# MoBA and MLA mixers on Trainium2: the last head group's values computed per token tile, and paired score products kept together

## The chip, the core and the metric

The kernel runs on one NeuronCore of a Trainium2 chip. The metric is the device time of one execution in microseconds (us); lower is better. The median of three timed runs before the change is 1003.63 us (1003.06 to 1005.63).

The engines are called by the profile's short names: PE (TensorE, matrix products; PEld is its weight load), DVE (VectorE), ACT (ScalarE), POOL (GpSimd) and SP (SyncE, which issues the DMAs here).

## What is computed

A trunk of two layers over one sequence of 256 tokens, width 1024, all in f32. Each layer is half a SwiGLU feed-forward, a token mixer, and half a feed-forward; layer 0 mixes with MoBA attention, layer 1 with MLA attention. Every sub-layer norms its input and shifts, scales and gates it by vectors made from `c`.

```python
def reference(x, c, positions, ...):
    c_act = silu(c)
    for layer in range(2):
        sh1, sc1, g1, sh2, sc2, g2, sh3, sc3, g3 = split(c_act @ ada_w[layer] + ada_b[layer], 9)
        h = modulate(rms_norm(x, norm_g[layer, 0]), sh1, sc1)
        x = x + 0.5 * g1 * swiglu(h, w_gate, w_up, w_down)
        h = modulate(rms_norm(x, norm_g[layer, 1]), sh2, sc2)
        mix = moba_attention(h, ...) if layer == 0 else mla_attention(h, ..., shared_k, shared_v)
        x = x + g2 * mix
        h = modulate(rms_norm(x, norm_g[layer, 2]), sh3, sc3)
        x = x + 0.5 * g3 * swiglu(h, ...)
    return x
```

With 256 tokens and a MoBA block of 256 both mixers come to causal attention over 16 heads: scores of a query with the keys (MoBA adds a position bias), softmax, a weighted sum of the values (64 wide), and an output projection of 1024 by 1024. MoBA's queries and keys are 64 wide, MLA's 96.

## The kernel before

**Numbers and tiles.** The 256 tokens are two token tiles of 128, t0 and t1. Every f32 operand of a large product is held as two fp32r parts, `hi` (a rounded copy) and `lo` (the rest), and a product is three matmuls added up in PSUM: hi by hi (L758), hi by lo (L759) and lo by hi (L760), in `mm3`. Weights come by DMA from SP into `raw` tiles of 1 MB (three buffers, L735); ACT copies each half into `hi` (L628) and DVE subtracts to get `lo` (L629), in `split`. `hi` and `lo` have eight buffers each, so a new `hi` can be written when the matmuls of the one eight places before have read it. The vectors from `c` are made beside this from `adaw` tiles, on DVE (L639, L677).

PSUM's eight banks are four accumulators `mm`, three banks for transposes, scores and values (`tr` and `at`, one pool), and one (`ada`) that MoBA's scores use as a fourth.

**Attention.** `attention()` runs once for each of the four groups of four heads (NG = 4, GH = 4) of either mixer. `scores` multiplies queries and keys; in MoBA (the branch with a bias) the four heads' products go, by token tile and by even and odd head, into four banks (`sides`, L1024). An even head's queries use the first 64 rows of the array and an odd head's the other 64. DVE adds the bias and takes the extreme (L1039), ACT does the exponential (L1046), DVE divides by the sum (L1051, L1052). `transposes` turns the probabilities (L1061): one unit of four transposes for t0 and two units for t1, each into one bank that ACT copies out as `pT` (L1063). `av` multiplies with the values (L1081) into one bank for both token tiles, and `split_evac` takes that out as the `hi` (ACT, L773) and `lo` (DVE, L774) parts of `oT`, two of the eight row blocks (k) of the out projection's input.

**Out projection and what follows.** `out_proj` has four accumulators, one for each token tile and half of the columns. In MoBA `mm_657` and `mm_659` are the two halves of t0, `mm_658` and `mm_660` those of t1. The last two row blocks (k = 6, 7) of each need the last group's `oT`. When one is complete, `resid` multiplies it with the gate and adds it to x (DVE, L868 and L869), and `stat` adds up squares (ACT L787, DVE L790). When both halves of a tile are done POOL makes `rstd`, ACT scales x into `y` (L803), PE transposes y (L808), ACT modulates it (L826) and `split_evac` makes the `hi` and `lo` of `h` (L773, L774), the input of the next feed-forward, whose first matmul needs them.

**What sets the order.** The program is written in rough order with continuations (`later(S_WAIT, ...)`, `later(PT_WAIT, ...)`, `later(AV_WAIT, ...)`), and then `class Order` (L243) schedules it: it simulates all engines with a table of costs, places one instruction after the other on the engine that is free first, takes on PE the oldest one that has been ready for a while (`choose`), and pins the result. Each engine then runs its instructions in exactly that order, waiting where an input or a buffer isn't there. So a change in one place can move instructions on all engines.

Of the kernel before, what the change touches and what calls it, by code (L numbers as in the profile page):

```python
# [24 lines left out]
S = 256  # L25
NT = S // P
# [5 lines left out]
DH = 64  # L32
# [210 lines left out]
class Order:  # L243
# [1 line left out]

    def __init__(self, nc, tc, rank, held, late, anchor):
        self.tc, self.rank, self.held = tc, rank, held
        self.tiles = {t.name: t for t in tc.info.tiles}  # L250
        self.ins, self.pre, self.aps = [], [], []
        self.uses, self.opened = {}, {}
        closed, seen, masks = [], {}, {}
        for i in nc.cur_bb.bb.instructions:
            kind = type(i).__name__
            if kind == "BassTilePoolBoundary":
                if i.op == "release":
                    closed.append(i.bass_pool_name)
                else:
                    self.opened[i.bass_pool_name] = list(closed)  # L260
            elif kind != "InstRegisterMove":
                self.add(i, seen, masks)
        n = len(self.ins)
        self.eng = [i.engine.name for i in self.ins]
        self.dma = [type(i).__name__ == "InstDMACopy" for i in self.ins]
        self.cost = [duration(i, a) for i, a in zip(self.ins, self.aps)]
        self.table = [{"Silu": "s", "Sin": "s", "Exp": "e"}.get(str(getattr(i, "func", "")).rsplit(".", 1)[-1])
                      if e == "Activation" else None for i, e in zip(self.ins, self.eng)]
        self.succ, self.after = [[] for _ in range(n)], [[] for _ in range(n)]
        self.npre = [len(p) for p in self.pre]  # L270
        for j, p in enumerate(self.pre):
            for i in p:
                self.succ[i].append(j)
        index = {i.name: k for k, i in enumerate(self.ins)}
        for x in late:
            if x in index:
                self.after[index[anchor]].append(index[x])
                self.npre[index[x]] += 1

        self.ring, self.bufs, self.rings, self.next_tile = {}, {}, {}, {}  # L280
        self.tiles_of = [[] for _ in range(n)]
        pools = {p.name: p for p in tc.info.pools}
        for name, us in self.uses.items():
            t = self.tiles[name]
            if t.space == DRAM:
                continue
            tag = str(t.tag).rsplit("_", 1)[0]
            pool = max((p for p in pools if tag.endswith("_" + p)), key=len)
            r = self.ring[name] = pool, tag
            if r not in self.bufs:  # L290
                self.bufs[r] = pools[pool].tag_meta[tag[:-len(pool) - 1]].bufs
            l = self.rings.setdefault(r, [])
            if l and self.uses[l[-1]][0] != us[0]:
                self.after[self.uses[l[-1]][0]].append(us[0])
                self.npre[us[0]] += 1
            if len(l) >= self.bufs[r]:
                self.next_tile[l[-self.bufs[r]]] = name
            l.append(name)
            for u in us:
                self.tiles_of[u].append(name)  # L300
# [63 lines left out]
    def place(self, need):  # L364
# [29 lines left out]
        def consider(k):  # L394

            r = ready[k]
            for t in self.tiles_of[k]:
                if t not in granted:
                    waiting.setdefault(t, []).append(k)
                    if t not in asked:  # L400
                        asked[t] = True
                        grant(self.ring[t])
                    return
                r = max(r, granted[t] + (WAKE if granted[t] else 0.0))
            if self.ins[k].name in self.held:
                r = max(r, HELD)
            ready[k] = r
            heapq.heappush(known[self.eng[k]], (r, k))

        def choose(e, t):  # L410
            av = avail[e]
            if e == "PE":
                first = min(av)
                old = [x for x in av if x[2] <= t - (GATE_MARGIN if x[0] < 0 else MARGIN)]
                x = min(old) if old else min(av, key=lambda x: (x[0] < 0, x))
                if x is not first and first[2] <= t and order[e] and order[e][-1] in self.pre[first[1]]:
                    x = first
                return x
            x = min(av)
            for r, j in known[e]:  # L420
                if r < t + min(self.cost[x[1]][0], SOON) and need[j] < x[0] - 500.0:
                    fit = [y for y in av if t + self.cost[y[1]][0] <= r + 60.0]
                    if fit:
                        return min(fit)
                    if need[j] < t + 3000.0:
                        free[e] = r
                        return None
                    break
            return x
# [93 lines left out]
def trunk(ctx: ExitStack, tc: tile.TileContext, a: dict, out: bass.AP):  # L523
# [28 lines left out]
    def later(us, fn):  # L552
        uid[0] += 1
        bisect.insort(pend, (clock[0] + us, uid[0], fn))
# [24 lines left out]

    first_rank, held, late, last_ffn = {}, set(), set(), []

    @contextmanager
    def noted(names):
# [289 lines left out]
    def kslice(tile_, k):  # L875
        return tile_[:, k * P:(k + 1) * P]
# [124 lines left out]
    def attention(ap, g, qTs, kTs, vs, bias, oT, state, after_s=None):  # L1001
# [7 lines left out]
        def scores():  # L1009
            until(lambda: state.get("av", 0) >= g)  # L1010
            banks = []
            if bias is None:
                for t, es in us:
                    ps3 = at_tile().rearrange("p (e k) -> p e k", k=P * (t + 1))
                    for i, e in enumerate(es):
                        nc.tensor.matmul(ps3[:, i, :], qTs(e, t), kTs(e, P * (t + 1)), start=i == 0, stop=False)  # L1016
                    nc.tensor.matmul(ps3[:, :, t * P:], ident_b, mask[:, :len(es)], start=False, stop=True)
                    banks.append([ps3[:, i, :] for i in range(len(es))])
            else:
                sides = [at_tile() for _ in range(3)] + [ps_ada.tile([P, 512], F32, tag="ada", name=nm("at"))]  # L1020
                sides = [x.rearrange("p (e k) -> p e k", k=P * (i // 2 + 1)) for i, x in enumerate(sides)]
                for t in range(NT):
                    for e in range(GH):
                        nc.tensor.matmul(sides[2 * t + e % 2][:, e // 2, :], qTs(e, t), kTs(e, P * (t + 1)),  # L1024
                                         start=True, stop=True)
                banks = [[sides[2 * t + e % 2][:, e // 2, :] for e in es] for t, es in us]
            pe(3.0)
            mxs = []
# [27 lines left out]
        def transposes():  # L1056
            for u, (t, es) in enumerate(us):
                pt = at_tile()
                for i, e in enumerate(es):
                    for kb in range(t + 1):  # L1060
                        nc.tensor.transpose(kslice(pt, i * (t + 1) + kb), ss[u][:, i, kb * P:(kb + 1) * P], ident)  # L1061
                w = ap.tile([P, 512], F32, tag="w", name=nm("pT"), bufs=5)
                nc.scalar.activation(w, pt, AF.Copy)  # L1063
                for i, e in enumerate(es):
                    for kb in range(t + 1):
                        pT[t, e, kb] = kslice(w, i * (t + 1) + kb)
            pe(1.4)
            state["p"] = g + 1
            if after_s:
                after_s()  # L1070
            later(AV_WAIT, av)

        def av():
            until(lambda: state.get("v", 0) > g)
            po = at_tile().rearrange("p (r t q) -> p r t q", r=GH // 2, t=NT)
            for pr in range(GH // 2):
                for t in range(NT):
                    for i in range(2):
                        e = 2 * pr + i
                        for kb in range(t + 1):  # L1080
                            nc.tensor.matmul(po[i * DH:(i + 1) * DH, pr, t, :], vs(e, kb),  # L1081
                                             pT[t, e, kb], start=kb == 0, stop=kb == t)
            pe(2.4)
            kk = g * (GH // 2)
            pov = po.rearrange("p r t q -> p t r q")
            hi, lo = [oT[0][3][:, kk:kk + 2, i].rearrange("p r t q -> p t r q") for i in range(2)]
            split_evac(hi, lo, pov)
            for t in range(NT):
                oT[t][2].update((kk, kk + 1))
            state["av"] = g + 1  # L1090

        later(S_WAIT, scores)

# [538 lines left out]
    mla(dict(hnext), hkv, norm_to((1, 2)))  # L1632
    ffn(1, 1, dict(hnext), lambda t: None, 18)
    drain()
    Order(nc, tc, first_rank, held, late, last_ffn[0]).apply()


# [17 lines left out]
```

## Time and profile before

| | us |
|---|---|
| median of three timed runs | 1003.63 |
| lowest and highest of them | 1003.06, 1005.63 |
| the profiled execution, its own time | 1006.99 |
| span of that profile, first to last instruction | 1005.2 |

The profile is one execution, 3.36 us above the median of the timed runs; 1.8 us of its time lie outside the span. Its views are: the busy time of each engine; the waits of an engine, by what released it; the chain of waits, which follows what ended last backwards through time (each row: start, length, engine and line; a length there is the step from one instruction's start to the next, not its latency); the timeline of an engine, instruction by instruction, with the idle time before each in brackets; and windows, which give each engine's busy time and the clock that PE was granted in a stretch of time. Durations in the timeline overlap for matmuls, since they are pipelined: a 128x512 matmul is listed with 0.39 us but the next one starts 0.23 us later. An f32 product is run as two passes over its columns, so that 8 score products of a group are 16 entries in the profile.

### The profile page before, as it was taken

The page shows a single profiled execution, that of the slowest core. Times are in us where ns is not written, and L with a number is a line of the kernel's source. Part 1 is how long each engine was busy: PE and PEld are TensorE (multiplying, and loading weights), DVE is VectorE, ACT ScalarE, POOL GpSimd, SP SyncE. Part 2 cuts the span into 40 slices and gives each one's busy share as a digit, 9 for nine tenths or more (in the row PEclk, how much of TensorE's full clock was granted, in tenths as well). Part 3 has the DMA queues.
Part 4 walks back from the last instruction along what each step waited for, and adds up shares of the span by engine and source line. Part 5 has one row for each costly group of instructions (what it writes and reads, how often), then busy time and mean ns, then how long its engine had stood idle before and what let it go on. Part 6 is the DMA issues. An engine that isn't in the chain of part 4 may idle for free.

```text
span 1005.2 us, 15142 instructions
## 1 busy us (share of the span) xinstructions
PE 986.0 (98%) x5558; PEld 834.1 (83%) x5558; DVE 844.9 (84%) x1389; ACT 616.7 (61%) x1111; POOL 83.8 (8%) x120
## 2 busy tenths in 40 slices
PE   8999999999999999999999999999989999999998
PEld 6988788877777788888888888888878878888886
DVE  7999999799989899999889999744998789667642
ACT  5689565378666775555367555643879686556421
POOL 2012000022231000000000000000143110000000
PEclk9999999999999999999999999999999999999999
DMA  9979879798886789988988998552344467544630
GB/s 352 404 283 304 317 285 360 299 336 328 273 292 246 254 294 329 340 326 291 364 310 331 341 334 300 180 210 104 105 152 149 144 227 283 204 168 168 224 132 21
DMA packets 54235, 260.51 MB, mean 259 GB/s; under 512 B 6289, under 2 KB 6801, under 8 KB 35986
## 3 DMA queue, kind: packets, MB, share of 16 engines
q1 hardware_dynamic: 52850, 256.06, 70.3%
q0 software_dynamic: 1024, 3.17, 1.1%
q8 instruction: 43, 0.70, 0.3%
q10 hardware_dynamic: 288, 0.33, 0.1%
q14 instruction: 30, 0.25, 0.1%
HBM read 255.34 MB, written 4.19 MB: 258 GB/s over the span
## 4 chain that ended last, share of the span: by engine, by line
PE 76%; issue 11%; DMA 6%; DVE 5%; ACT 2%; POOL 1%; SPq 0%; POOLq 0%; ACTq 0%; DVEq 0%
PE mm L955 20%; PE mm L758 13%; PE mm L759 13%; PE mm L760 13%; PE mm L962 11%; DMA adaw<-in_ada_dram 2%; DMA bias_d<-bt 2%; DMA raw<-in_first_dram 1%; PE at L1081 1%; DVE lo L629 1%; PE at L1016 1%; PE at L1024 1%; PE tr L808 1%; DMA raw<-in_w_dram 1%; PE at L1061 1%
## 5 line engine op out<-in xcount | busy, mean ns | idle before, releaser
L629 DVE TENSOR_TENSOR lo<-raw,hi 128x1024 fp32r<-128x1024 f32 (+3 forms) x312 | 371.4, 1201 | 86.8 <-ACT hi L628 67.6
L628 ACT ACTIVATE hi<-raw 128x1024 fp32r<-128x1024 f32 (+3 forms) x312 | 316.4, 1039 | 153.9 <-PE mm L760 113.6
L955 PE MATMUL mm<-h,hi 128*128 128x512 f32 x1120 | 288.3, 394 | 2.5 <-DVE ry L967 1.8
L955 PEld LDWEIGHTS mm<-h,hi 128*128 128x128 f32 x1120 | 199.7, 189 | 37.8 <-DVE ry L967 2.1
L962 PEld LDWEIGHTS mm<-h,lo 128*128 128x128 f32 x1120 | 155.3, 190 | 11.9
L962 PE MATMUL mm<-h,lo 128*128 128x256 f32 x1120 | 162.0, 283 | 0.0
L639 DVE CUSTOM_DVE_ANT_0 adaw<-adaw,c_b,cols 128x1024 f32<-128x1024 f32 x112 | 141.6, 1279 | 1.6 <-DMA adaw<-in_ada_dram 1.6
L758 PE MATMUL mm<-hi,gh 128*128 128x512 f32 x352 | 137.3, 390 | 0.0
L760 PE MATMUL mm<-hi,gl 128*128 128x512 f32 x352 | 137.1, 389 | 0.0
L759 PE MATMUL mm<-lo,gh 128*128 128x512 f32 x352 | 137.0, 389 | 0.0
L966 ACT ACTIVATE both<-mm 128x256 f32<-128x256 f32 x108 | 40.6, 376 | 91.0 <-PE mm L962 90.6
L758 PE MATMUL mm<-hi,h 128*128 128x512 f32 (+1 forms) x240 | 94.9, 401 | 0.8 <-ACT h L773 0.8
L760 PE MATMUL mm<-hi,h 128*128 128x512 f32 (+1 forms) x240 | 93.5, 394 | 1.6 <-DVE h L774 1.6
L759 PE MATMUL mm<-lo,h 128*128 128x512 f32 (+1 forms) x240 | 94.9, 397 | 0.0
L760 PEld LDWEIGHTS mm<-hi,gl 128*128 128x128 f32 x352 | 66.1, 188 | 13.7
L759 PEld LDWEIGHTS mm<-lo,gh 128*128 128x128 f32 x352 | 66.1, 188 | 13.5
L758 PEld LDWEIGHTS mm<-hi,gh 128*128 128x128 f32 x352 | 66.1, 188 | 13.4
L677 DVE SCALAR_TENSOR_TENSOR acc<-adaw,cols,acc 128x1024 f32<-128x1024 f32 x48 | 61.5, 1280 | 0.1
L967 DVE TENSOR_TENSOR both<-both,mm 128x256 f32<-128x256 f32 x108 | 44.9, 416 | 14.4 <-ACT both L966 14.0
L760 PEld LDWEIGHTS mm<-hi,h 128*128 128x128 f32 x240 | 45.5, 190 | 10.4 <-DVE h L774 2.1
L758 PEld LDWEIGHTS mm<-hi,h 128*128 128x128 f32 x240 | 45.4, 189 | 9.7 <-ACT h L773 1.3
L759 PEld LDWEIGHTS mm<-lo,h 128*128 128x128 f32 x240 | 45.3, 189 | 9.0 <-issue 1.0
(234 smaller groups left out, 1182.7 us busy)
## 6 DMA issues: line engine op xcount, KB each, us to landing
raw<-in_w_dram SPq DMA_DIRECT2D x142, 1024.0 KB, 5.7
adaw<-in_ada_dram SPq DMA_DIRECT2D x160, 512.0 KB, 5.7
raw<-in_first_dram SPq DMA_DIRECT2D x24, 256.0 KB, 7.3
raw<-in_w_dram SPq DMA_DIRECT2D x12, 512.0 KB, 3.9
raw<-in_w_dram SPq DMA_DIRECT2D x6, 576.0 KB, 4.1
bias_d<-bt SPq DMA_DIRECT2D x12, 256.0 KB, 5.2
bg<-bias_d POOLq DMA_DIRECT2D x4, 768.0 KB, 7.6
raw<-in_w_dram SPq DMA_DIRECT2D x2, 768.0 KB, 4.1
```

Of the source, the lines that this page charges most:

```text
L628: nc.scalar.activation(hi, src, AF.Copy)
L629: nc.vector.tensor_tensor(lo, src, hi.bitcast(F32), op=ALU.subtract)
L639: nc.vector.tensor_tensor_reduce(wt, wt, c_b, 1.0, cols[:, i, c:c + 1], op0=ALU.mult, op1=ALU.add, accum_out=m_cols[:, i, c:c + 1])
L677: nc.vector.scalar_tensor_tensor(acc, ada_tile(j, k), cact[:, k:k + 1], acc, op0=ALU.mult, op1=ALU.add)
L758: nc.tensor.matmul(ps, lh, rh, start=start, stop=False)
L759: nc.tensor.matmul(ps, lh, rl, start=False, stop=False)
L760: nc.tensor.matmul(ps, ll, rh, start=False, stop=stop)
L808: nc.tensor.transpose(kslice(pt, j), kslice(y, j), ident)
L955: nc.tensor.matmul(ps, wh, hk_both(h, k).rearrange("p i t q -> p (i t q)"), start=k == 0, stop=False)
L962: nc.tensor.matmul(ps[:, S:], wl, hk_both(h, k)[:, 0].rearrange("p t q -> p (t q)"), start=False, stop=k == KD - 1)
L966: nc.scalar.activation(sums, ps[:, S:], AF.Copy)
L967: nc.vector.tensor_tensor(sums, sums, ps[:, :S], op=ALU.add)
```

## The change

It has two parts.

1. **Twins.** In MoBA's scores each odd head's product is tied to that of the even head before it. `Order` lets the even one wait for everything that the odd one needs, its PSUM tile too, and places the odd one right behind it on PE.
2. **The last group's values by token tile.** In the last group (g = NG - 1) of both mixers `av` is run twice: for t0 directly behind t0's transposes and its `pT` copy, and for t1 where `av` stood. Each has an `at` bank of its own and a `split_evac` of half the width, so that t0's row blocks 6 and 7 are marked as there before t1's transposes are written.

```diff
@@ Order.__init__
-    def __init__(self, nc, tc, rank, held, late, anchor):
+    def __init__(self, nc, tc, rank, held, late, anchor, twins):
...
         index = {i.name: k for k, i in enumerate(self.ins)}
+        self.twin = {index[a]: index[b] for a, b in twins}
+        for a, b in self.twin.items():
+            for i in self.pre[b] - self.pre[a] - {a}:
+                self.pre[a].add(i)
+                self.succ[i].append(a)
+                self.npre[a] += 1
@@ Order, consider(k)
-            for t in self.tiles_of[k]:
+            for t in self.tiles_of[k] + (self.tiles_of[self.twin[k]] if k in self.twin else []):
@@ Order, choose(e, t)
                 first = min(av)
+                if order[e] and order[e][-1] in self.twin:
+                    b = self.twin[order[e][-1]]
+                    for x in av:
+                        if x[1] == b:
+                            return x
+                    for r, j in known[e]:
+                        if j == b:
+                            free[e] = r
+                            return None
@@ attention(), scores()
                         nc.tensor.matmul(sides[2 * t + e % 2][:, e // 2, :], qTs(e, t), kTs(e, P * (t + 1)),
                                          start=True, stop=True)
+                        if e % 2:
+                            twins.append([i.name for i in nc.cur_bb.bb.instructions[-2:]])
@@ attention(), transposes()
                     for kb in range(t + 1):
                         pT[t, e, kb] = kslice(w, i * (t + 1) + kb)
+                if g == NG - 1 and u == 0:
+                    av([0])
             pe(1.4)
             state["p"] = g + 1
             if after_s:
                 after_s()
-            later(AV_WAIT, av)
+            later(AV_WAIT, lambda: av([1] if g == NG - 1 else [0, 1]))
 
-        def av():
+        def av(ts):
             until(lambda: state.get("v", 0) > g)
-            po = at_tile().rearrange("p (r t q) -> p r t q", r=GH // 2, t=NT)
+            n = len(ts)
+            po = at_tile()[:, :n * S].rearrange("p (r t q) -> p r t q", r=GH // 2, t=n)
             for pr in range(GH // 2):
-                for t in range(NT):
+                for j, t in enumerate(ts):
                     for i in range(2):
                         e = 2 * pr + i
                         for kb in range(t + 1):
-                            nc.tensor.matmul(po[i * DH:(i + 1) * DH, pr, t, :], vs(e, kb),
+                            nc.tensor.matmul(po[i * DH:(i + 1) * DH, pr, j, :], vs(e, kb),
                                              pT[t, e, kb], start=kb == 0, stop=kb == t)
-            pe(2.4)
+            pe(1.2 * n)
             kk = g * (GH // 2)
-            pov = po.rearrange("p r t q -> p t r q")
-            hi, lo = [oT[0][3][:, kk:kk + 2, i].rearrange("p r t q -> p t r q") for i in range(2)]
-            split_evac(hi, lo, pov)
-            for t in range(NT):
+            hi, lo = [oT[0][3][:, kk:kk + 2, i, ts[0]:ts[-1] + 1].rearrange("p r t q -> p t r q") for i in range(2)]
+            split_evac(hi, lo, po.rearrange("p r t q -> p t r q"))
+            for t in ts:
                 oT[t][2].update((kk, kk + 1))
-            state["av"] = g + 1
+            if ts[-1]:
+                state["av"] = g + 1
```

`twins` is passed through to `Order(nc, tc, first_rank, held, late, last_ffn[0], twins)`. The lines move by up to 20: the score product of L1024 becomes L1039, L1061 becomes L1078, L1081 becomes L1101, `mm3` L773 to L775, the `hi` split L643, `split_evac` L788 and L789, `y` L818.

How the order changes is shown at three places. The first is PE at the scores of MoBA's last group (tiles `at_685` and `at_686` are t0's even and odd heads, `at_687` and `at_688` t1's). Before:

```order
L1024 MATMUL at_685_3697<-kT_680_3666,qT_2786 128x128
L1024 MATMUL at_688_3700<-kT_680_3666,qT_2786 128x256
L1024 MATMUL at_686_3698<-kT_680_3666,qT_2786 128x128
L758 MATMUL mm_658_3596<-hi_621_3472,oT_2787 128x512
L1024 MATMUL at_685_3697<-kT_680_3666,qT_2786 128x128
L1024 MATMUL at_686_3698<-kT_680_3666,qT_2786 128x128
L1024 MATMUL at_687_3699<-kT_680_3666,qT_2786 128x256 x2
L1024 MATMUL at_688_3700<-kT_680_3666,qT_2786 128x256
```

and after the change:

```order
L1039 MATMUL at_685_3697<-kT_680_3666,qT_2786 128x128
L1039 MATMUL at_686_3698<-kT_680_3666,qT_2786 128x128
L1039 MATMUL at_685_3697<-kT_680_3666,qT_2786 128x128
L1039 MATMUL at_686_3698<-kT_680_3666,qT_2786 128x128
L1039 MATMUL at_688_3700<-kT_680_3666,qT_2786 128x256
L1039 MATMUL at_687_3699<-kT_680_3666,qT_2786 128x256 x2
L1039 MATMUL at_688_3700<-kT_680_3666,qT_2786 128x256
```

In the first list an even product of t0 is followed by an odd one of t1, an odd one of t0 and a large matmul; in the second the even and odd head of one tile stand side by side in all four pairs, and the large matmul has left. The other three groups of MoBA have the same two patterns.

The second place is PE between the transposes and the values of the same group, where `pT_709` belongs to t0 and `at_715` holds the values of both tiles. Before, from the last transposes on:

```order
L1061 MATMUL at_712_3789<-ident_90,s_693_3719 128x128 x4
L760 MATMUL mm_660_3598<-hi_662_3601,oT_2787 128x512
L1081 MATMUL at_715_3796<-pT_709_3780,v_559_3235 64x128 x2
L1081 MATMUL at_715_3796<-pT_711_3787,v_559_3235 64x128 x2
L758 MATMUL mm_660_3598<-hi_664_3605,oT_2787 128x512
L758 MATMUL mm_658_3596<-hi_667_3623,oT_2787 128x512
L1081 MATMUL at_715_3796<-pT_713_3794,v_559_3235 64x128 x2
L1081 MATMUL at_715_3796<-pT_709_3780,v_559_3235 64x128 x2
L1081 MATMUL at_715_3796<-pT_711_3787,v_559_3235 64x128 x2
L1081 MATMUL at_715_3796<-pT_713_3794,v_559_3235 64x128 x2
L759 MATMUL mm_660_3598<-lo_665_3606,oT_2787 128x512
```

and after, from the values of t0 (`at_710`) to those of t1 (`at_723`), the first five rows:

```order
L1101 MATMUL at_710_3782<-pT_709_3780,v_559_3235 64x128 x4
L1078 MATMUL at_711_3789<-ident_90,s_691_3715 128x128 x4
L1078 MATMUL at_713_3796<-ident_90,s_693_3719 128x128 x4
L775 MATMUL mm_660_3598<-hi_664_3605,oT_2787 128x512
L773 MATMUL mm_660_3598<-hi_664_3605,oT_2787 128x512
```

and, nine matmuls on, the values of t1 with what ends t0's second half:

```order
L775 MATMUL mm_659_3597<-hi_705_3761,oT_2787 128x512
L1101 MATMUL at_723_3834<-pT_712_3794,v_559_3235 64x128 x2
L1101 MATMUL at_723_3834<-pT_714_3801,v_559_3235 64x128 x2
L1101 MATMUL at_723_3834<-pT_712_3794,v_559_3235 64x128 x2
L1101 MATMUL at_723_3834<-pT_714_3801,v_559_3235 64x128 x2
L773 MATMUL mm_659_3597<-hi_705_3761,oT_2787 128x512
L774 MATMUL mm_659_3597<-lo_706_3762,oT_2787 128x512
L775 MATMUL mm_659_3597<-hi_705_3761,oT_2787 128x512
L774 MATMUL mm_660_3598<-lo_665_3606,oT_2787 128x512
```

The values of t0 have moved ahead of t1's transposes, and t0's k = 6, 7 matmuls (`mm_657` and `mm_659` with weights `hi_669` and `hi_705`) stand ahead of and around the values of t1. From the last `mm_659` matmul to the first y transpose there were 17 matmuls before, and there are 22 now.

The third place is ACT where the out projection ends (`hi_...` from `raw_...` are weight splits for the next feed-forward, `y_727` and `y_728` the first scaled x of t0). Before:

```order
L773 ACTIVATE oT_2787<-at_715_3796 128x2x2x128
L628 ACTIVATE hi_760_3968<-raw_757_3962 128x1024
L628 ACTIVATE hi_763_3986<-raw_762_3984 128x1024
L787 ACTIVATE ry_716_3817,ssq0_717_3820<-x0_101 128x512
L628 ACTIVATE hi_765_3990<-raw_762_3984 128x1024
L628 ACTIVATE hi_771_4021<-raw_770_4019 128x1024
L628 ACTIVATE hi_773_4025<-raw_770_4019 128x1024
L803 ACTIVATE y_727_3853<-x0_101,rstd_726_3851 128x256
L803 ACTIVATE y_729_3855<-x0_101,rstd_726_3851 128x256
L826 ACTIVATE y_727_3853<-tr_737_3888,m_cols_104 128x128
L773 ACTIVATE h_725_3850<-y_727_3853 128x128
```

and after:

```order
L802 ACTIVATE ry_716_3809,ssq0_717_3812<-x0_101 128x512
L788 ACTIVATE oT_2787<-at_723_3834 128x2x128
L643 ACTIVATE hi_761_3971<-raw_758_3965 128x1024
L643 ACTIVATE hi_764_3989<-raw_763_3987 128x1024
L643 ACTIVATE hi_766_3993<-raw_763_3987 128x1024
L818 ACTIVATE y_728_3856<-x0_101,rstd_727_3854 128x256
L818 ACTIVATE y_730_3858<-x0_101,rstd_727_3854 128x256
L818 ACTIVATE y_732_3860<-x0_101,rstd_727_3854 128x256
L841 ACTIVATE y_728_3856<-tr_738_3891,m_cols_104 128x128
L788 ACTIVATE h_726_3853<-y_728_3856 128x128
L841 ACTIVATE y_728_3856<-tr_738_3891,m_cols_104 128x128
L841 ACTIVATE y_730_3858<-tr_741_3912,m_cols_104 128x128
```

The first two y's stood behind the splits of `raw_770` and now stand ahead of those of the same tile (`raw_771` in the second list), which have moved behind the h's of t0; a third y stands ahead of the first modulation.

More of the change, by code (lines that the diff above doesn't have):

```diff
@@ L578, in drain @@
             run_next()
-    first_rank, held, late, last_ffn = {}, set(), set(), []
+    first_rank, held, late, last_ffn, twins = {}, set(), set(), [], []
     @contextmanager
@@ L1634, in trunk @@
     drain()
-    Order(nc, tc, first_rank, held, late, last_ffn[0]).apply()
+    Order(nc, tc, first_rank, held, late, last_ffn[0], twins).apply()
 def kernel(**inputs):
```

## The prediction

> **What bounds the kernel now.** I read the page first, then PE's waits, then windows over the stages that the change touches.
>
> ```profile
> PE 986.0 (98%) x5558; PEld 834.1 (83%) x5558; DVE 844.9 (84%) x1389; ACT 616.7 (61%) x1111; POOL 83.8 (8%) x120
> ```
>
> PE is busy for 98% of the span. A part of the change pays only if it takes time off PE itself, or off one of PE's few waits. Its waits, by line and releaser (us in total, how many, the longest):
>
> ```profile
> PE tr L808 <- ACT y L803: 1.8, 2, 1.5
> PE tr L1453 <- DVE kn L1488: 0.8, 2, 0.6
> PE mm L758 <- ACT h L773: 0.8, 2, 0.6
> ```
>
> The first and the third have their longest occurrence behind MoBA's out projection. The second lies in MLA between its groups. MoBA's attention itself is full:
>
> ```profile
> 244.00:260.00 16.00, 16.00 (x99) 12.55 (x98) 14.06 (x36) 13.38 (x29) 4.83 (x3) 1.00 0.82 288
> 260.00:290.00 30.00, 30.00 (x165) 24.04 (x164) 27.62 (x54) 17.26 (x34) 5.92 (x4) 1.00 0.85 297
> 290.00:312.00 22.00, 22.00 (x134) 17.49 (x132) 19.99 (x40) 14.40 (x31) 6.26 (x3) 1.00 0.77 263
> 312.00:332.50 20.50, 20.48 (x115) 15.76 (x113) 18.43 (x39) 13.07 (x29) 0.00 (x0) 1.00 0.66 236
> ```
>
> The columns are the window's length, then the busy time of PE, PEld, DVE, ACT and POOL, the granted clock, and the DMA share. In 88.5 us PE is busy for all but 0.02, and DVE for 14.06 + 27.62 + 19.99 + 18.43 = 80.1, which is 91%. So here PE's own work is the bound, with DVE close behind it.
>
> **Part 1, the score pairs.** The chain of waits has MoBA's first group, and later its last:
>
> ```profile
> 245.04 0.85 PE at L1024 x5
> 245.90 0.43 PE mm L758
> 246.33 1.28 PE at L1024 x10
> ...
> 312.25 0.85 PE at L1024 x5
> 313.10 0.43 PE mm L758
> 313.54 1.28 PE at L1024 x10
> 314.82 0.43 PE mm L759
> 315.25 0.24 PE mm L760
> ```
>
> All four groups read so. Three products take 0.85, a large matmul caught between them 0.43 where its likes take 0.23 or 0.24, and five products 1.28: 2.56 us, of which 0.23 is the matmul's own work. In the new order the eight stand in four pairs, and the matmul stands elsewhere. The ten passes of the x10 row show the price of pairs. They hold one pair of t0 and three products of t1, two of an even head and one of an odd. The even half of the array streams 2 x 128 + 4 x 256 = 1280 columns in 1.28 us, 1.0 ns a column with its start, and the odd half has room beside it. The three products that join are t1's second odd one, which fits into that room, and a second pair of t0, two passes of 128 columns: 0.26 us. So 1.28 + 0.26 + 0.23 = 1.77 replaces 2.56. That is **-0.79 us a group, -3.2 us in four**. If the added pair costs nothing it is 4 x 1.05 = -4.2; if the odd product finds room for half of its 2 x 256 columns only, another 0.26 a group is lost and it is -2.1. I take -3.2, because in the x10 row an odd product already runs in that room.
>
> PE's work in this stage covers the softmax chain. What has to be late for PE to wait? The last group's products ended at 314.82 and its first transposes came at 318.49, with 15 large matmuls between. Now there are 16, so the chain behind the products has 0.23 us more, and t0's bank is complete earlier inside the run. That cover doesn't shrink. What does shrink is the time for DVE's other work (splits, `adaw` columns), for which there is a rival below.
>
> **Part 2 in MoBA: transposes and values.**
>
> ```profile
> 307.77 1.51 PE at L1081 x24
> ...
> 318.49 0.44 PE at L1061 x4
> ...
> 321.19 0.80 PE at L1081 x8
> 321.99 0.66 PE mm L758 x2
> 322.65 1.24 PE at L1081 x16
> 323.89 0.43 PE mm L759
> ```
>
> The third group does its 24 value passes in 1.51. The last group took 0.80 + 1.24 = 2.04 in two pieces, because a transposed tile was late, and its x8 piece mixed t0 with one head of t1. Each piece is followed by a matmul of 0.43, 0.20 above 0.23. Now the pieces are t0 (8 passes) and t1 (16), each whole pairs, so I take 1.51 plus 0.1 for a second start. The t0 piece is followed by transposes, which keep their 0.44 for four, so one of the two breaks goes too. Sum: 2.04 - 1.61 = 0.43 and something of the 0.20. **I take -0.5**, between -0.2 (the pieces cost what they did, one break goes) and -0.75. The second `split_evac` adds an ACT and a DVE instruction of half width. On ACT it stands behind `pT_709` and two weight splits (1.06 each, by a row below), so its `hi` comes some 3.2 us after t0's transposes. PE has six matmuls (1.4), the values (0.5), eight transposes (0.9) and three matmuls (0.7) until it reads that `oT`: 3.5 us. It just fits, and I take nothing; a split that comes late uses the cover up, and then PE waits for as long as it is late.
>
> **Part 2 in MoBA: the wait behind the out projection.**
>
> ```profile
> 332.25 0.24 PE mm L760
> 332.51 1.06 ACT hi L628
> 333.57 0.41 ACT y L803
> 334.02 0.45 PE tr L808 x2
> 334.56 0.47 ACT y L826
> 335.05 0.32 ACT h L773
> 335.41 0.55 PE mm L758
> ...
> 332.51 1.06 ACT L628 ACTIVATE hi<-raw 128x1024 fp32r<-128x1024 f32 x1 [0.30 <-PE mm L760]
> ...
> 329.09 1.22 DVE L629 TENSOR_TENSOR lo<-raw,hi 128x1024 fp32r<-128x1024 f32 x1
> 330.23 0.68 DVE L868 TENSOR_TENSOR ry<-mm,gate 128x512 f32<-128x512 f32 x1
> ...
> 332.35 0.08 DVE L790 DVE_READ_ACCUMULATOR2_ANT ssq<- 128x1 f32 x1
> ...
> 332.52 0.55 POOL L795 TENSOR_TENSOR rstd<-ssq,mhalf 128x1 f32<-128x1 f32 x1 [25.11 <-DVE ssq L790]
> ```
>
> PE stops when its last out-projection matmul is done (332.5) and waits 1.5 for `y`, then 0.6 for `h` (the longest of the two rows of waits above): 2.1 us. Two things are late at once. `rstd` is there only at 333.07, and ACT is in a weight split that waited for the buffer freed by the very last matmul. The new order cuts both. The t0 accumulator is complete 22 matmuls ahead of the transposes instead of 17. DVE started on that accumulator at 330.23, behind a split of 1.22, and its squares ended at 332.4, after which POOL's 0.55 gives `rstd`; in the new order that split stands behind the squares. And ACT's last split ahead of `y` (`hi_766`) now waits for the matmul that has four others behind it (0.9 us). So y is ready 1.06 + 0.41 + 0.05 = 1.5 after that matmul, and PE idles 1.5 - 0.9 = 0.6. Behind it the third pair of transposes and a matmul fill most of the second wait; about 0.3 stays. **From 2.1 to 0.9: -1.2 us.** Ends: -2.1 (no wait left), and 0 (something else is late by as much).
>
> **Part 2 in MLA.** There the values stood together, and PE waited on nothing near them:
>
> ```profile
> 798.36 1.31 PE at L1061 x12
> ...
> 800.59 1.51 PE at L1081 x24
> ```
>
> The split only adds: a second start (0.1) and a second break (0.20) at the values, and a break (0.1) as the transposes part into 4 and 8. By the order, 20 large matmuls lie between t0's accumulator and the first y transpose instead of 23; at 0.23 they are 4.6 us, above the 332.4 + 0.55 + 0.41 - 330.23 = 3.1 that MoBA's chain from residual to y takes by the rows above, so nothing new waits there. **+0.4 us**, between +0.2 (one break) and +0.7 (0.80 + 1.24 as in MoBA instead of 1.51, and one break).
>
> **What the scheduler moves besides.** In MLA between the groups the `kn` transposes now come in one run, and two DVE splits stand behind `kn` that stood ahead of it, while one score unit comes seven matmuls later. The waits there are 0.8 us in all. They may go (-0.8), or a wait of seven matmuls (1.6) may come. **I take -0.3**, nearer to the row of 0.8. The feed-forwards are reordered in places, but in the same full PE.
>
> **Sum:** -3.2 - 0.5 - 1.2 + 0.4 - 0.3 = **-4.8 us**. On the profiled execution, 1006.99 (span 1005.2), that is 1002.2. The median of the timed runs stands 3.36 lower, so 1003.63 - 4.8 = **998.8 us**.
>
> **The clock.** The profiled execution has something that the timed ones need not have:
>
> ```profile
> 328.90:332.31 3.41, 3.41 (x16) 1.00 0.79 244
> 332.31:335.72 3.41, 1.31 (x6) 1.00 0.25 106
> 335.72:339.13 3.41, 3.41 (x11) 0.50 0.91 298
> 752.14:755.56 3.42, 1.97 (x14) 1.00 0.00 0
> ```
>
> The wait behind MoBA's out projection left PE busy for 1.31 of 3.41 us, and the granted clock was halved for the next 3.41: 1.7 us lost. A stretch with 1.97 busy was not followed by it. With 0.9 idle, 2.5 of 3.41 stay busy and the halving should go. The stretches' ends needn't fall alike in each execution, so I leave these 1.7 us out of the median's sum; with them the profiled execution would come to 1000.5. [...]
>
> **Rivals.**
>
> 1. *Only the pairs pay.* The wait for `y` stays 2.1, because another split or the later DVE order holds it, and MLA's moved score unit costs 0.6: -3.2 - 0.5 + 0.4 + 0.6 = -2.7, so 1000.9. For it: DVE has an `adaw` column newly between t0's two residuals, on a tile as large as that of the 1.22 row. Against it: PE still works at `mm_659` then. Chance 0.18.
> 2. *The pairs don't overlap*, as a semaphore comes between their halves: -1.6 is left, 1002.0. For it: four banks must all be free at once. Against: the pair in the x10 row runs so. Chance 0.06.
> 3. *DVE becomes the bound of MoBA's attention: slower.* Its 80.1 us have to fit into what was 88.5 and becomes about 84.8. If it can keep busy only as in the first window, 14.06 of 16.00 or 0.88, the stage takes 80.1 / 0.88 = 91.0, which is +2.5 instead of -3.7; with -1.2 and +0.1 for the rest that gives 1005.0. The point from which the kernel is slower is 80.1 / 89.6 = 0.89. Against it: PE waited for DVE nowhere here, and DVE reached 0.92 in the second window (27.62 of 30.00), which would still leave 87.0 and a gain of 2.6. Chance 0.08.
> 4. *More*: the median had a halved clock too, or the first two terms lie at their far ends: 994 to 996.6. Chance 0.11.
>
> **The numbers.** The forecast, 996.6 to 1000.5 about 998.8, has the 0.57 left. A range of 996.0 to 1002.2 leaves out most of rival 3, half of 4 and a little of 2: about 0.16. A measurement of this kernel can't tell less than 0.3%, 3.0 us, from no change. Below 1000.6 lie the forecast, rival 4 and a few of 1: faster 0.70. Above 1006.6 lies a part of rival 3: slower 0.06. The same: 0.24.
>
> **What would show it.** Right: MoBA's sixteen score passes in a row of about 1.5 us in the chain, all four groups; value pieces near 0.5 and 1.1; PE's wait `tr L808 <- ACT y` under 1; no halved clock near 332. Wrong: new waits of PE for DVE between 240 and 330 (rival 3), score passes over 2 us (rival 2), a wait of 1.5 still there (rival 1).

## The result, and the profile after

| | us |
|---|---|
| median of five timed runs with the change | 995.87 (995.11 to 999.07) |
| median of five runs of the kernel before, beside them | 1005.26 (1003.06 to 1005.73) |
| ratio | 0.9916, 95% interval 0.9903 to 0.9929 |
| span of the profile with the change | 994.1 |

The change makes the kernel 0.84% faster, 8.4 us of 1005 (7.1 to 9.7). The forecast was 4.8 us, 998.8; the median lies just below the range's lower end of 996.0.

From the page of the changed kernel, busy time by engine:

```profile
PE 979.9 (99%) x5558; PEld 831.1 (84%) x5558; DVE 844.2 (85%) x1391; ACT 615.5 (62%) x1113; POOL 77.7 (8%) x120
```

And its waits of PE (us in total, how many, the longest):

```profile
PE tr L1473 <- ACT s L1063: 1.6, 2, 1.4
...
PE mm L773 <- ACT h L788: 0.5, 2, 0.3
PE tr L823 <- ACT y L818: 0.2, 1, 0.2
PE tr L1473 <- DVE kn L1508: 0.2, 1, 0.2
```

PE was busy for 986.0 before and is for 979.9 now. The wait of 1.5 for `y` is gone (the 0.2 left is at another place), the longest for `h` has halved, and the longer of the two waits for `kn` in MLA is gone. The wait of 1.8 for `ry` ahead of MoBA is gone too, though every engine's order is the same there; more of that below.

The chain of waits of the changed kernel, at MoBA's first group, at the transposes of its second, and in its last:

```profile
243.07 1.51 PE at L1039 x16
244.58 0.43 PE mm L773
...
269.21 0.87 PE at L1078 x8
...
307.96 1.51 PE at L1039 x16
309.47 0.43 PE mm L774
...
315.16 0.59 PE at L1101 x8
315.75 1.02 PE at L1078 x8
...
319.53 1.07 PE at L1101 x16
320.61 0.43 PE mm L773
```

All sixteen score passes stand in one run of 1.51. The values take 0.59 and 1.07. The 0.20 that the first break cost is gone at the matmul, but the eight transposes that follow the values take 1.02, where the eight of the second group take 0.87; so most of it comes back there.

The timeline of the changed kernel behind the out projection, ACT, POOL and PE:

```profile
324.50 1.06 ACT L643 ACTIVATE hi<-raw 128x1024 fp32r<-128x1024 f32 x1 [0.49 <-PE mm L775]
325.47 1.29 ACT L818 ACTIVATE y<-x,rstd 128x256 f32<-128x256 f32 x3
...
323.91 0.55 POOL L810 TENSOR_TENSOR rstd<-ssq,mhalf 128x1 f32<-128x1 f32 x1 [20.83 <-DVE ssq L805]
...
326.35 0.60 PE L823 MATMUL tr<-ident,y 128*128 128x128 f32 x4
327.02 0.38 PE L823 MATMUL tr<-ident,y 128*128 128x128 f32 x2
327.68 0.50 PE L773 MATMUL mm<-hi,h 128*128 128x512 f32 x1 [0.28 <-ACT h L788]
```

The y transposes have no idle time before them. `rstd` was there at 324.46, 1.9 us ahead of them, and the split in front of `y` began at 324.50, when a matmul was done that had nine others between it and the transposes.

DVE stayed clear of being the bound. This is the sum line of four windows over MoBA's attention (242 to 325 us) of the changed kernel:

```profile
sum 83.00, PE 83.00 PEld 66.50 DVE 78.01 ACT 56.06 POOL 16.47; mean PE 20.75 PEld 16.62 DVE 19.50 ACT 14.02 POOL 4.12
```

PE works in every microsecond, with DVE at 78.01 / 83.00 = 94%.

**Three stretches** make profiles comparable. They are cut at the start of MoBA's first score product (244.97 in the profile before), at the first y transpose behind MoBA's out projection (334.02), at the first y transpose ahead of MLA (706.85), and at the end of the span; what comes before the first cut is left out. In us, from the rows of each profile:

| kernel | MoBA | behind it, and two feed-forwards | MLA and the rest |
|---|---|---|---|
| before | 89.05 | 372.83 | 298.3 |
| before, a second profile | 89.04 | 372.68 | 298.3 |
| with the change | 83.35 | 370.95 | 296.8 |
| twins alone | 86.19 | 372.83 | 297.9 |
| twins, split in MoBA only | 83.35 | 371.07 | 298.5 |
| twins, split in MLA only | 86.17 | 372.92 | 296.2 |
| full change, twins of the same half | 87.12 | 371.82 | 296.5 |
| twins alone, matmuls in the wait | 86.16 | 371.78 | 297.9 |
| MoBA's split, MLA's scores 1.0 later | 83.35 | 371.05 | 297.1 |
| MoBA's split, MLA's values 1.0 later | 83.35 | 370.98 | 298.3 |
| full change, MLA's scores 1.0 later | 83.35 | 371.05 | 298.0 |
| MoBA's split, MLA's scores 2.0 later | 83.37 | 371.06 | 297.6 |

With the change the three are -5.7, -1.9 and -1.5 us: 9.1 in the profile, beside 8.4 in the timed runs.

### The profile page after: what moved, and what is told of

Its sections match the earlier page's. It is cut to its first block, busy times and chain, and to the rows that moved or that the text cites. A ratio compares the mean times of both kernels' runs of the same rounds, so it can differ in the third digit from the quotient of the medians.

```text
span 994.1 us, 15134 instructions
## 1 busy us (share of the span) xinstructions
PE 979.9 (99%) x5558; PEld 831.1 (84%) x5558; DVE 844.2 (85%) x1391; ACT 615.5 (62%) x1113; POOL 77.7 (8%) x120
## 4 chain that ended last, share of the span: by engine, by line
PE 73%; DVE 10%; issue 10%; DMA 4%; ACT 2%; POOL 1%; SPq 0%; DVEq 0%; ACTq 0%; POOLq 0%
PE mm L970 21%; PE mm L773 12%; PE mm L775 12%; PE mm L774 12%; PE mm L977 11%; DVE lo L644 3%; DMA raw<-in_w_dram 2%; PE at L1101 1%; PE at L1078 1%; DMA adaw<-in_ada_dram 1%; PE tr L823 1%; DVE oh L1221 1%; DMA raw<-in_first_dram 1%; ACT hi L643 1%; DVE acc L692 1%
## 5 line engine op out<-in xcount | busy, mean ns | idle before, releaser
L643 ACT ACTIVATE hi<-raw 128x1024 fp32r<-128x1024 f32 (+3 forms) x312 | 315.8, 1038 | 157.9 <-PE mm L775 115.8
L773 PE MATMUL mm<-hi,gh 128*128 128x512 f32 x352 | 137.3, 390 | 0.0
L775 PE MATMUL mm<-hi,gl 128*128 128x512 f32 x352 | 137.1, 389 | 0.0
L773 PE MATMUL mm<-hi,h 128*128 128x512 f32 (+1 forms) x240 | 94.5, 400 | 0.5 <-ACT h L788 0.5
L775 PE MATMUL mm<-hi,h 128*128 128x512 f32 (+1 forms) x240 | 92.4, 391 | 1.4 <-DVE h L789 1.4
L775 PEld LDWEIGHTS mm<-hi,gl 128*128 128x128 f32 x352 | 66.1, 188 | 13.7
L773 PEld LDWEIGHTS mm<-hi,gh 128*128 128x128 f32 x352 | 66.1, 188 | 13.4
L775 PEld LDWEIGHTS mm<-hi,h 128*128 128x128 f32 x240 | 45.0, 188 | 10.3 <-DVE h L789 1.7
L773 PEld LDWEIGHTS mm<-hi,h 128*128 128x128 f32 x240 | 45.1, 188 | 10.1 <-issue 1.2
```

What stands on the lines that cost most here:

```text
L643: nc.scalar.activation(hi, src, AF.Copy)
L773: nc.tensor.matmul(ps, lh, rh, start=start, stop=False)
L775: nc.tensor.matmul(ps, ll, rh, start=False, stop=stop)
```

## The experiments

The letters A to J are the theories and rivals that the expectations name.

### The parts one by one

The twins alone: `transposes` and `av` as before.

```diff
-                if g == NG - 1 and u == 0:
-                    av([0])
...
-            later(AV_WAIT, lambda: av([1] if g == NG - 1 else [0, 1]))
+            later(AV_WAIT, lambda: av([0, 1]))
```

> The twins alone; the values of the last group stay together in both mixers. Theory A, that the parts add up as the two traces read (pairs -3.3 us, values and the wait behind MoBA's out projection -2.2 and -1.7 of clock, MLA -1.5): 3.3 us faster than before, a wait of 1.5 for y still there, MLA unchanged. Rival B, that the pairs only take the place of waits that the split of the values makes possible to remove: under 1.5 us faster, with new waits of PE in MoBA.

Measured: 1001.72, ratio 0.9968 (0.9955 to 0.9980), so 3.2 us faster. MoBA's stretch is 2.86 shorter. The four runs of scores give 4 x 0.82 = 3.3 (2.56 before; 1.51 and 0.23 for the matmul that left), and 0.5 is lost again in the wait for `y`, which has become 2.0:

```profile
PE tr L823 <- ACT y L818: 2.3, 2, 2.0
```

The timeline of the same kernel, ACT and POOL at that place:

```profile
325.21 2.95 ACT L643 ACTIVATE hi<-raw 128x1024 fp32r<-128x1024 f32 x3
...
327.87 0.56 POOL L810 TENSOR_TENSOR rstd<-ssq,mhalf 128x1 f32<-128x1 f32 x1 [24.84 <-DVE ssq L805]
328.46 0.91 ACT L818 ACTIVATE y<-x,rstd 128x256 f32<-128x256 f32 x2 [0.30 <-POOL rstd L810]
```

ACT's last split ended at 328.16, and `rstd` was there at 328.43: it came last, by 0.27, where before the change the split came last, by 0.50 (333.57 and 333.07). So without the split of the values both things are late; by these rows, having the later one in time would alone bring no more than 0.3 here, and 0.5 before the change. Theory A stands but for the length of the wait, B falls.

The split in MoBA only, with the twins (`bias` is there in MoBA alone); the split in MLA only is the same edit with `bias is None`:

```diff
-                if g == NG - 1 and u == 0:
+                if bias is not None and g == NG - 1 and u == 0:
...
-            later(AV_WAIT, lambda: av([1] if g == NG - 1 else [0, 1]))
+            later(AV_WAIT, lambda: av([1] if bias is not None and g == NG - 1 else [0, 1]))
```

> Twins, and the values split by token tile in MoBA only; MLA's order is that of before. Theory A: 3.3 + 2.2 = 5.5 us faster than before, 7.2 where the halved clock behind the out projection fell on the run before; no wait for y; MLA takes as long as before from 741 us on. Rival C, that MLA's 1.5 us in the trace are a difference between two executions, as the 2.0 us ahead of MoBA must be (the order is the same there): as fast as the full change.

Measured: 998.7, ratio 0.9932 (0.9919 to 0.9946), 6.8 us faster, between A's 5.5 and 7.2. MoBA's stretch falls by another 2.84, of which 2.04 is the whole wait for `y`; the rest lies in smaller pieces at the last groups. The stretch behind falls by 1.8. MLA stays at 298.5, and its `kn` wait of 0.6 is there. So C falls: MLA's gain comes with the other half of the change.

> Twins, and the values split in MLA only; up to MLA this is the order of the twins alone, in MLA that of the full change. Theory A: 1.5 us faster than the twins alone, all of it between the first score products of MLA and the last values, with the kn wait of 0.6 gone. My own prediction of before, in which the split costs MLA 0.4 and the scheduler gives 0.3: the same as the twins alone. Rival C: no difference either, with the 1.5 us gone in this profile.

Measured: 1000.68, ratio 0.9952 (0.9939 to 0.9964), 1.0 us less than the twins alone by the medians; the intervals of the two ratios overlap. The profile is plainer: the first two stretches are those of the twins alone, and MLA's is 296.2 against 297.9. Theory A stands: MLA gains. My forecast of no gain there is wrong.

### What a pair is

The twins tie heads that use the same half of the array (the profile lists a score product as `64*128`):

```diff
-                        if e % 2:
-                            twins.append([i.name for i in nc.cur_bb.bb.instructions[-2:]])
+                        if e >= 2:
+                            last = nc.cur_bb.bb.instructions
+                            twins.append([last[-3].name, last[-1].name])
```

> The full change, but the twins tie heads 0 and 2 and heads 1 and 3, which use the same half of the array: the eight products of a group still stand in one run without a large matmul between them. Theory A, that the gain is the overlap of an even with an odd head: the run takes 2.3 to 2.5 us instead of 1.51 and some 3.2 to 3.8 us of the change's gain are lost. Rival D, that it is the uninterrupted run: 1.5 us for the sixteen passes, and the gain stays within 0.8 us.

Measured: 1001.18, ratio 0.9960 (0.9948 to 0.9973); 4.4 us of the change's 8.4 are lost, somewhat more than A's 3.2 to 3.8; MoBA's stretch is 3.8 longer than with the change, and the one behind it 0.9, though PE has no wait left there. The scheduler did not keep one run, contrary to what I expected; a large matmul stands in it. From the chain of waits of this kernel, first group:

```profile
244.03 1.52 PE at L1039 x10
245.54 0.43 PE mm L773
245.97 1.06 PE at L1039 x4
247.03 0.43 PE mm L774
```

The first row is six products (twelve passes, of which the chain follows ten), the second the two that are left. Six products without an interruption take 1.52, as long as eight in even and odd pairs. So it is the pairing that counts, and D falls. With 1.52 + 1.06 these are even slower than before the change (0.85 + 1.28). The same eight products take 1.51 with the halves in turn and 1.52 + 1.06 in this order.

### The clock behind the wait

Eight matmuls that nobody reads fill the wait of the twins-alone kernel, pinned right ahead of the first y transpose; nothing else in the order differs.

```diff
+                if half and t == 0 and gate_key == (0, 1):
+                    pf = ps_ada.tile([P, 512], F32, tag="ada", name="fill").rearrange("p (c q) -> p c q", q=P)
+                    for i in range(8):
+                        nc.tensor.matmul(pf, ones_r, ones_r[:, None, :].to_broadcast([P, 4, P]), start=i == 0, stop=i == 7)
```

> The twins alone, with eight large matmuls whose result nobody reads put on PE in the wait behind MoBA's out projection, right ahead of the first y transpose; the order is otherwise that of the twins alone. Theory E, that this wait halves the clock behind it in nearly every execution, as in the three profiles that have the wait: no halved clock near 330 us and 1.7 us faster than the twins alone, though PE waits for y until the same time. Rival F, that the halved clock is a matter of the profiled executions: the same time as the twins alone, within 0.5 us.

Measured: 1001.15, ratio 0.9963 (0.9951 to 0.9976), 0.6 us less than the twins alone, with intervals that overlap almost wholly: the times alone can't tell E from F. The clocks can. Windows of the twins alone, then of the kernel with the filled wait (length, PE busy, granted clock, DMA share, GB/s):

```profile
327.29:330.70 3.41, 1.13 (x5) 1.00 0.29 112
330.70:334.11 3.41, 3.41 (x11) 0.50 0.76 264
```

```profile
327.20:330.60 3.40, 3.10 (x14) 1.00 0.44 157
330.60:334.00 3.40, 2.74 (x12) 1.00 0.56 154
```

The clock stays whole (1.00 in both windows), and the stretch behind MoBA is 371.78 instead of 372.83: 1.05 us, not 1.7. Where the other 0.6 went is shown in part only: PE now waits 0.2 for the `lo` part of `h`:

```profile
332.46 0.49 PE L781 MATMUL mm<-hi,h 128*128 128x512 f32 x1 [0.22 <-DVE h L795]
```

How often a timed run had it can be read, nearly, from the mean clock that each lists: one halved window of 3.4 us takes 0.0017 off it in a run of 1000 us. The kernels with the idle wait (before, twins alone, split in MLA only) list 0.998 or less in 18 of 27, two of five and four of five runs. The kernels without it, the filled one among them, do so in one run of 39, which is the 999.07 of the change. So the halved clock belongs to the wait in the timed runs too, though not in "nearly every execution" as E has it, and F falls.

Its price is less certain than its cause. The 18 runs before have a median of 1005.4, the other nine one of 1003.9, which would be 1.5 us; of the twins alone, the three runs without it (1001.68 to 1002.24) are no faster than the two with it (1001.53 and 1003.40). With the 1.05 of the profiles I put it at 1.0 to 1.5.

How busy PE was ahead of a halved clock and of a whole one is shown by windows of this length in other profiles. The split in MLA only, which has the same wait as the twins alone:

```profile
328.65:332.07 3.42, 1.39 (x6) 1.00 0.27 109
332.07:335.48 3.41, 3.41 (x10) 0.50 0.90 283
```

The kernel before, at its wait of 1.8 for `ry`, where the clock did not fall:

```profile
117.27:120.68 3.41, 1.86 (x12) 1.00 0.76 250
120.68:124.10 3.42, 3.19 (x14) 1.00 0.79 273
```

And the changed kernel, in MLA, where it did not fall either:

```profile
741.82:745.23 3.41, 1.82 (x14) 1.00 0.00 0
745.23:748.65 3.42, 3.30 (x25) 1.00 0.19 24
```

### Whether MLA's gain belongs to the split

MLA's values stay together; its scores are written 1.0 us of the planner's clock later, and in the second kernel its values:

```diff
-        later(S_WAIT, scores)
+        later(S_WAIT if bias is not None else S_WAIT + 1.0, scores)
```

```diff
-            later(AV_WAIT, lambda: av([1] if bias is not None and g == NG - 1 else [0, 1]))
+            later(AV_WAIT if bias is not None else AV_WAIT + 1.0, lambda: av([1] if bias is not None and g == NG - 1 else [0, 1]))
```

> Twins and the split in MoBA only (so MLA's values are not split), but MLA's scores are written 1.0 us of the planner's clock later, which reorders MLA's instructions and changes nothing else. Theory G, that the 1.6 us which MLA gained are what a reshuffle by the scheduler happened to give, not a gain of the split: MLA moves by anything between -1.6 and +1.6 us against the kernel with the split in MoBA only. Rival H, that the split of MLA's values is what brings it: the same as that kernel or slower, kn wait of 0.6 still there.

> As the run before, with MLA's values instead of its scores written 1.0 us later. Theory G: another change of MLA's time, of either sign, within 1.6 us of the kernel with the split in MoBA only. Rival H: the same as that kernel or slower.

Measured: 997.23, ratio 0.9920 (0.9907 to 0.9934), and 997.85, ratio 0.9930 (0.9918 to 0.9943), against 0.9932 of the same kernel without the edit. Scores later bring MLA from 298.5 to 297.1 and the `kn` wait goes, without any split there: H falls for this run. Values later bring nothing beyond the spread of that stretch (297.9 to 298.5 in the five profiles with MLA's old order), as H had it, and the wait is there:

```profile
PE tr L1473 <- DVE kn L1508: 0.8, 2, 0.6
```

> The full change, with MLA's scores written 1.0 us later as well. Theory G, that MLA's gain is a matter of which order the scheduler falls into: the two gains of 1.6 (split of MLA's values) and 1.4 us (scores later) don't add; MLA ends within 1 us of the full change, on either side. Rival I, that they are two separate waits that each removes: 1.2 to 1.5 us faster than the full change.

> Twins and the split in MoBA only, with MLA's scores written 2.0 us later instead of 1.0. Theory G: MLA's time differs again from that of 1.0, without a rule; between 0 and 2 us faster than with the split in MoBA only. Rival J, that later scores are a gain in themselves: at least the 1.4 us that 1.0 brought, and the kn wait of 0.6 gone again.

The edits are the same line in the full change, and with 2.0 in the kernel with MoBA's split only. Measured: 997.61, ratio 0.9922 (0.9909 to 0.9936), and 997.29, ratio 0.9923 (0.9910 to 0.9937). The two gains don't add: MLA takes 298.0, more than with either alone. With 2.0 it takes 297.6, and a new wait of 1.0 for `v` stands where the one for `kn` went:

```profile
PE mm L773 <- ACT v L1510: 1.0, 1, 1.0
```

Rivals I and J fall. G stands in kind: these edits make the scheduler fall into different orders of MLA, worth 0 to 2 us. Its bound for the full change, within 1 us, was passed (298.0 against 296.8). No version beat the full change.

What the split itself does to MLA is in the chain of waits of the changed kernel, at MLA's last group:

```profile
787.20 0.44 PE at L1078 x4
...
789.26 0.59 PE at L1101 x8
789.85 1.03 PE at L1078 x8
...
793.40 1.07 PE at L1101 x16
```

Before the change the twelve transposes took 1.31 and the values 1.51, each in one piece. They now take 0.44 + 1.03 = 1.47 and 0.59 + 1.07 = 1.66. So the split itself costs MLA 0.3, and the gain comes from what the scheduler moved besides.

### The kernel before once more

> The kernel before once more, for a second profile of it. If the 2.0 us that the two first profiles differ by ahead of MoBA, where the order is the same, belong to single executions, the wait of 1.8 us at 119 us has another length here, and the halved clock near 335 us is there again by theory E.

Measured: 1005.58 in one run. The span is 1003.8 against 1005.2, and the wait for `ry` at 119 us is 0.7 long. In the ten other profiles, all with the same order there, it is between 0 and 1.6. The halved clock is there again:

```profile
330.50:333.88 3.38, 1.62 (x8) 1.00 0.23 95
333.88:337.29 3.41, 3.07 (x7) 0.50 0.70 233
```

## Why the prediction was right, and where it was too small

- **Score pairs, -3.2: right.** 4 x 0.82 = 3.3. The run took 1.51 where the sum had 1.28 + 0.26 = 1.54.
- **Values and transposes in MoBA, -0.5: about right** by the pieces: 0.59 and 1.07 against 0.5 and 1.1, which is 0.38 less than before. Of the break of 0.20, 0.15 came back in the transposes behind the values, which "keep their 0.44 for four" in the sum. That makes -0.4.
- **Wait behind the out projection, 2.1 to 0.9: right in kind, too small.** It went to 0.28. The step that failed is the one on `hi_766`, "now waits for the matmul that has four others behind it": the buffer came free at a matmul with nine others behind it, so `y` was there before PE wanted it. The twins alone bear out "two things are late at once": there `rstd` came last, 0.27 behind the splits, and PE waited 2.0.
- **The clock: wrongly left out.** "I leave these 1.7 us out of the median's sum" cost 1.0 to 1.5. Each of the four profiles with the wait has the halved clock behind it (mean clock 0.997 or 0.998), and none of the eight without (0.999 or 1.0); by their mean clock so have 24 of 37 timed runs with it, against one of 39 without. The reason given, that the stretches need not fall alike in each execution, is not shown for the timed runs, as those have no trace; the two profiles of the kernel before, with the same waits of 1.5 and 0.6, have 1.31 and 1.62 us of PE in the window ahead of the halved clock. About a third of the runs with the wait list no halving. By their times, two of the three runs shown beforehand, 1003.06 and 1003.63, lie with that third; I took them for the usual case.
- **MLA, +0.4 - 0.3: wrong sign.** It gained 1.5. The +0.4 for the split was about right, 0.3 by its rows. The step that failed is the -0.3 for "what the scheduler moves besides", which was near -1.8: the waits for `kn` (0.6), `lo` (0.3) and `h` (0.2) went, which "they may go (-0.8)" had in part, and the order moved also where PE was busy. Nothing here tells beforehand what an order gives: MLA's stretch ranges from 296.2 to 298.5 over the orders that the scheduler found for these edits.
- **Sum.** -4.8 becomes -3.3 - 0.4 - 1.8 - 1.5 = -7.0 with the measured terms, and -8.0 to -8.5 with the clock, against 8.4 (7.1 to 9.7) timed. The three stretches of the profiles have 9.1; 0.4 of it in MoBA and about 0.6 behind it have no term here.
- **Rivals.** That DVE becomes the bound fell: it reached 94% with no wait of PE. The sixteen passes of the twins took 1.51, not rival 2's over 2, and the wait for `y` went. The time is that of rival 4, more, and a part of its reason came true, the clock. But MLA's 1.6 beyond the forecast stood in no rival, so that 995.87 lies in its 994 to 996.6 is partly luck.

The clock fell after windows with 1.13, 1.31, 1.39 and 1.62 us busy of 3.4, in four profiles of four that had this wait; after 1.82, 1.86 and 1.97 it did not. So the windows ahead of a halved clock were not idle as a whole. In the kernel before, two waits of 2.1 us together (1.5 and 0.6) were enough, and the one of 1.8 for `ry` was not.

## What to carry to other kernels

Price a product that uses half of the array by its neighbour: here eight took 1.51 us with the halves in turn, and six took 1.52 where products of the same half were tied. So check what the instruction order puts side by side, not only what is ready. Where waits leave PE idle, look at the granted clock behind them as well: here it halved for 3.4 us behind windows with 1.13 to 1.62 us busy of 3.4, and stayed whole behind those with 1.82 to 1.97. Count it as often as the mean clocks of the timed runs show it. And where a list scheduler sets the order, an edit moves code far from its place: measure that part with an unrelated edit before you credit the change with it.

## What was not expected of the hardware

The same instructions in the same order waited for `ry` at 119 us between 0 and 1.8 us, from one execution to the next, and for `s` ahead of MLA's first groups, in five profiles of one order, between 0.5 and 1.4. Of the 1.4 us between the spans of the two profiles of the kernel before, the wait for `ry` is 1.1. So differences between profiles were read by stretches here. Whether these waits also make the spread of 1 to 4 us between timed runs of one kernel isn't shown, as those have no trace, and why the waits differ was not tried.
